# A hybrid diffusion layer: the first stage in two passes, scaled x times v0 and modulated x times v1

## The chip, the cores and the metric

The kernel runs on one core of a Trainium2 chip. The metric is the device time of one execution in microseconds; lower is better. All data is fp32; large products are split by hand into two parts of a rounded type, so each takes three products on TensorE (PE).

## The reference

One layer of a bidirectional backbone over 640 tokens (128 context tokens and 512 latent ones) of width 2048, with a conditioning vector for each of the two groups. The part in question is the beginning:

```python
sh1, sc1, g1, sh2, sc2, g2 = modulation(cond, w_mod, b_mod)    # silu(cond) @ w_mod + b_mod, cut into 6 pieces
u = rmsnorm(x, g_pre_mix) * (1.0 + sc1) + sh1
q, k, v, o, ig, fg, z, xbc, dt = split(u @ w_in)
```

After that come an mLSTM on four heads (it reads q, k, v and the gates ig, fg) and an SSD on 16 heads (it reads a 3x3 convolution of xbc, and dt), both in two directions over chunks of 128 tokens, an output projection, a second norm and modulation, and an MLP of width 8192 with squared ReLU.

## The kernel before, in words

Everything is kept with features on the partitions: x is 16 tiles k of 128 features x 640 tokens (`xT`, KT = 16). The modulated input u is held as `ah` (rounded) and `al` (what is left), so that a product is `ah*whi + ah*wlo + al*whi`. A weight block of 128x1024 (512 KB) is loaded by SyncE into `raw`, cast by ScalarE (ACT) into `whi` (L204), and its rest is formed by VectorE (DVE) into `wlo` (L205); `raw` has two buffers, `whi` and `wlo` three each.

The first stage (L293 to L353) does this:

- It loads x in eight DMAs of two tiles (L298), squares each tile on ACT (L300) and adds the squares on DVE into `rb` (L302). `norm_row` sums over partitions on PE, takes the root on GpSimd and spreads the result (L166 to L178, L304).
- `mod1(k)` (L315 to L330) makes scale and shift of tile k: two loads of 1 MB (L312), 16 products of 32x256 in four column groups of PE (L321), a copy (L325), two transposes and a sum (`mod_sum`, L258, L259), then scale `a1` (L329) and shift `modT` (L330).
- The loop over k (L335) forms u as x*a1*rb on DVE (L341), `ah` as u+shift on ACT (L342), `al` on DVE (L343), multiplies with the 48 gate columns (`mm_a` into `gps`, L217), and, after every second k, with two tiles of v0, the first 512 columns of v (`mm_b` into `vps`, L233 to L235: 30 products of 512 columns).

v0 and v1 are the two halves of v; v0 serves heads 0 and 1 of the mLSTM, v1 heads 2 and 3. After the stage the gate columns and v0 are copied out of PSUM (`gT` L404, `v_tile` L396), and the gate chain begins: small products on PE (L412 to L524) between many small operations on DVE and ACT, with a round trip through DRAM, up to `wk`, `dec` and `gu` (L509 to L512). Beside it PE does v1 by `proj_b` and q and k of head 0 by `proj_a`. Each weight block of those takes with it one `mod_step` (L261 to L279), which does a quarter of one of the other modulation pieces: a load into `mraw`, four products of 32x256 (L269), an addition. The mLSTM of head h (`mlstm`) begins with transposes of k (L590) and needs `wk` for `kw` (L593); q and k of the next head are projected beside it. The convolved tiles 8 and 12 of the SSD are projected between q, k of head 3 and its mLSTM.

The order on each engine is written out by a scheduler when the kernel is built, from the order of the program and the buffers of the pools; on the chip each engine follows it strictly.

## Time and profile before

| what | value |
| --- | --- |
| median of 3 runs | 2887.56 us (2886.55 to 2887.63) |
| profiled execution, its own time | 2888.12 us |
| its span in the profile | 2886.4 us, 48385 instructions |
| PE busy | 2833.0 us (98%) |
| DVE, ACT, POOL busy | 67%, 45%, 15% |
| granted TensorE clock, mean | 0.997 |
| DMA | 498.52 MB, mean 173 GB/s |

The page divides the span into 40 slices of 72 us. PE is full in all but the first, where it stands at 6 tenths; the DMA is at 9 tenths in that slice alone and in a short stretch late in the run. Products are pipelined, so a busy PE need not be at its peak: the time of a product is better read from the step between two starts than from its duration.

### The profile page before, as it was taken

The page shows a single profiled execution, that of the slowest core. Times are in us where ns is not written, and L with a number is a line of the kernel's source. Part 1 is how long each engine was busy: PE and PEld are TensorE (multiplying, and loading weights), DVE is VectorE, ACT ScalarE, POOL GpSimd, SP SyncE. Part 2 cuts the span into 40 slices and gives each one's busy share as a digit, 9 for nine tenths or more (in the row PEclk, how much of TensorE's full clock was granted, in tenths as well). Part 3 has the DMA queues.
Part 4 walks back from the last instruction along what each step waited for, and adds up shares of the span by engine and source line. Part 5 has one row for each costly group of instructions (what it writes and reads, how often), then busy time and mean ns, then how long its engine had stood idle before and what let it go on. Part 6 is the DMA issues. An engine that isn't in the chain of part 4 may idle for free.

```text
span 2886.4 us, 48385 instructions
## 1 busy us (share of the span) xinstructions
PE 2833.0 (98%) x18872; PEld 2631.7 (91%) x18872; DVE 1944.4 (67%) x3117; ACT 1286.1 (45%) x2312; POOL 419.3 (15%) x456
## 2 busy tenths in 40 slices
PE   6999999999999999999999999999999999999998
PEld 4679897888887889999999999999999999999997
DVE  4463464787765757677777666666776776677976
ACT  3322333233413423555444444444555556555364
POOL 0000000223211000000000000000005444443200
PEclk9999999999999999999999999999999999999999
DMA  9743434555647667555444333333448999997254
GB/s 364 291 137 115 141 120 134 176 167 159 207 144 226 240 228 264 206 182 168 161 158 138 113 108 114 110 109 108 163 128 182 213 204 191 196 214 178 88 208 157
DMA packets 211748, 498.52 MB, mean 173 GB/s; under 512 B 22424, under 2 KB 111768, under 8 KB 211008
## 3 DMA queue, kind: packets, MB, share of 16 engines
q1 hardware_dynamic: 153872, 429.38, 43.7%
q0 software_dynamic: 39792, 45.73, 10.1%
q10 hardware_dynamic: 17856, 20.32, 1.9%
q8 instruction: 148, 2.42, 0.3%
q14 instruction: 80, 0.66, 0.1%
HBM read 405.33 MB, written 44.97 MB: 156 GB/s over the span
## 4 chain that ended last, share of the span: by engine, by line
PE 92%; DVE 4%; DMA 3%; issue 1%; ACT 1%; DVEq 0%; SPq 0%; POOL 0%; ACTq 0%; POOLq 0%
PE mm L812 20%; PE mm L810 20%; PE mm L811 20%; PE mm L217 10%; PE mm L233 3%; PE mm L235 3%; PE mm L234 3%; PE tr L269 3%; PE mod L321 1%; DVE wlo L948 1%; PE vps L233 1%; DMA raw<-in_w 1%; PE vps L234 1%; PE ms L634 1%; PE vps L235 1%
## 5 line engine op out<-in xcount | busy, mean ns | idle before, releaser
L948 ACT CAST whi<-raw 128x512 fp32r<-128x512 f32 (+1 forms) x659 | 500.7, 767 | 584.1 <-PE mm L811 391.9
L948 DVE TENSOR_TENSOR wlo<-raw,whi 128x512 fp32r<-128x512 f32 (+1 forms) x659 | 574.8, 880 | 259.1 <-ACT whi L948 253.3
L810 PE MATMUL mm<-ah,whi 128*128 128x320 f32 x1536 | 477.8, 311 | 1.2 <-ACT whi L948 1.2
L812 PE MATMUL mm<-ah,wlo 128*128 128x320 f32 x1536 | 474.4, 310 | 4.2 <-DVE wlo L948 3.9
L811 PE MATMUL mm<-al,whi 128*128 128x320 f32 x1536 | 475.8, 310 | 0.0
L204 ACT CAST whi<-raw 128x1024 fp32r<-128x1024 f32 x162 | 169.3, 1047 | 405.9 <-PE mm L235 128.7
L810 PEld LDWEIGHTS mm<-ah,whi 128*128 128x128 f32 x1536 | 289.2, 188 | 9.8 <-issue 7.8
L812 PEld LDWEIGHTS mm<-ah,wlo 128*128 128x128 f32 x1536 | 288.6, 188 | 9.5 <-DVE wlo L948 4.7
L1229 POOL DMA_DIRECT2D pc<-ev x275 | 241.6, 905 | 365.2 <-ACT ev L1228 356.3
L811 PEld LDWEIGHTS mm<-al,whi 128*128 128x128 f32 x1536 | 289.2, 188 | 4.4 <-issue 4.1
L205 DVE TENSOR_TENSOR wlo<-raw,whi 128x1024 fp32r<-128x1024 f32 x162 | 202.0, 1248 | 132.3 <-ACT whi L204 131.9
L217 PE MATMUL mm<-ah,whi 128*128 128x256 f32 (+1 forms) x768 | 189.7, 319 | 0.0
L217 PE MATMUL mm<-al,whi 128*128 128x256 f32 (+1 forms) x768 | 188.9, 319 | 0.0
L217 PE MATMUL mm<-ah,wlo 128*128 128x384 f32 (+1 forms) x768 | 186.0, 316 | 0.0
L233 PE MATMUL mm<-whi,ah 128*128 128x512 f32 x400 | 161.6, 404 | 0.0
L234 PE MATMUL mm<-wlo,ah 128*128 128x512 f32 x400 | 160.0, 400 | 0.0
L235 PE MATMUL mm<-whi,al 128*128 128x512 f32 x400 | 159.5, 399 | 0.0
L810 PE MATMUL mm<-q,whi 128*128 128x320 f32 x512 | 157.7, 308 | 0.0
L812 PE MATMUL mm<-q,wlo 128*128 128x320 f32 x512 | 157.7, 308 | 0.0
L1228 ACT COPY ev<-mm 128x320 f32<-128x320 f32 x275 | 116.2, 425 | 65.4 <-DMA pc<-ev 46.2
L217 PEld LDWEIGHTS mm<-ah,whi 128*128 128x128 f32 x768 | 121.1, 188 | 10.2 <-issue 9.1
L217 PEld LDWEIGHTS mm<-ah,wlo 128*128 128x128 f32 x768 | 120.7, 188 | 6.9 <-issue 5.8
(419 smaller groups left out, 6692.6 us busy)
## 6 DMA issues: line engine op xcount, KB each, us to landing
raw<-in_w SPq DMA_DIRECT2D x460, 512.0 KB, 3.5
mraw<-in_w SPq DMA_DIRECT2D x128, 512.0 KB, 4.1
pc<-ev POOLq DMA_DIRECT2D x275, 160.0 KB, 4.9
m<-in_w SPq DMA_DIRECT2D x32, 1024.0 KB, 6.3
R<-hd SPq DMA_DIRECT2D x32, 640.0 KB, 7.0
xs<-csd SPq DMA_DIRECT2D x40, 256.0 KB, 5.0
hd<-s ACTq DMA_DIRECT2D x62, 160.0 KB, 2.9
hd<-u ACTq DMA_DIRECT2D x62, 160.0 KB, 1.9
```

The costliest lines, as they stand in the source:

```text
L204: S.copy(hi, t)
L205: V.tensor_sub(lo, t, hi)
L217: PE.matmul(ps[h][:, 0:HW[h]], lhsT=w[:, cs_], rhs=a[:, k, HS[h]], start=(k == 0 and i == 0), stop=(k == KT - 1 and i == 2))
L233: PE.matmul(ps[:, :], lhsT=ah[:, k, tok], rhs=hi[:, wc], start=first, stop=False)
L234: PE.matmul(ps[:, :], lhsT=ah[:, k, tok], rhs=lo[:, wc], start=False, stop=False)
L235: PE.matmul(ps[:, :], lhsT=al[:, k, tok], rhs=hi[:, wc], start=False, stop=last)
L810: PE.matmul(ps, lhsT=wh[:, c], rhs=bh[:, k, :], start=(start and k == 0), stop=False)
L811: PE.matmul(ps, lhsT=wh[:, c], rhs=bl[:, k, :], start=False, stop=False)
L812: PE.matmul(ps, lhsT=wl[:, c], rhs=bh[:, k, :], start=False, stop=(stop and k == nk - 1))
L948: newest[:] = S.copy(hi, src), V.tensor_sub(lo, src, hi)
L1228: S.copy(ev, ps)
L1229: G.dma_start(pi[:, j, :], ev, accum_op=OP.add)
```

## The change

The first stage becomes two passes over k, in pairs. Pass 1 needs only the scale: it multiplies x*a1, without the norm and without the shift, with v0, and the norm's factor of each token is put in when v0 leaves PSUM (`rc5`). The squares are formed in this pass, into one buffer. Pass 2 has the shift and the norm, forms u as before and multiplies it with v1; `ah` and `al` of all k come out of it for the later projections. The modulation blocks are laid out anew: a block row of 32 x 256 now holds 256 columns of scale (pass 1) or of shift (pass 2), loaded as four DMAs of 512 KB, with five buffers of `m1` and the two of `mraw`; x is loaded pair by pair. Shift's part of v0 is the same for all tokens of a group, so it is a product of the shift vector with the weights of v0: `v0_steps` loads the eight blocks of v0 a second time, forms it in steps that go beside the next projections (in place of `mod_step` there, which then runs later), and adds it to v0. The gate columns become a projection of their own after pass 2. The convolved tiles 8 and 12 are projected right after q and k of head 0. Line numbers with "L" in the rows of the change are its own.

```diff
@@ block_keys
-    for k in range(KT):
-        keys += [("m1", k, j) for j in range(4)]
-        if k % 8 == 0:
-            keys.append(("A", "g", 0, k // 8))
-        if k % 2 == 1:
-            keys.append(("B", "v", 0, k // 2))
-    keys += [("B", "v", 1, j) for j in range(8)]
+    for v in range(2):
+        for p in range(KT // 2):
+            keys += [("m1", v, p, j) for j in range(4)]
+            keys.append(("B", "v", v, p))
+    keys += [("A", "g", 0, j) for j in range(2)]
@@ proj_a, proj_b
-                if mod["n"] < MODCAP[0]:
-                    mod_step()
+                side_step()
...
+        def side_step():
+            if first:
+                if next(first[0], "end") == "end":
+                    first.pop()
+                else:
+                    return
+            if mod["n"] < MODCAP[0]:
+                mod_step()
...
-            for k in range(KT):
-                if k % 2 == 0:
-                    SY.dma_start(xT[:, k:k + 2, :], A["xT"][:, k * T:(k + 2) * T].rearrange("p (a b) -> p a b", b=T))
-                sq = rb if k == 0 else (wb, wp)[k % 2].tile([P, 1024], F32, tag=("raw", "mraw")[k % 2], name="sq", bufs=2)[:, 0:T]
-                S.activation(sq, xT[:, k, :], AF.Square)
-                if k:
-                    V.tensor_add(rb, rb, sq)
...
+            def load_m1(v, p):
+
                 r = []
-                for jj in range(2):
-                    w = p0.tile([P, 2, 1024], F32, tag="m1", name="m1", bufs=4)
...
+                for j in range(4):
+                    i = more["m1"] = more.get("m1", -1) + 1
+                    if i % 7 < 2:
+                        w = wp.tile([P, 1024], F32, tag="mraw", name="mraw", bufs=2)
+                    else:
+                        w = p0.tile([P, 1024], F32, tag="m1", name="m1", bufs=5)
+                    SY.dma_start(w, A["w"][BLK["m1", v, p, j]])
                     r.append(w)
                 return r
...
+            mod1(0, 0)
+            load_x(0)
+            for p in range(KT // 2):
+                vw = split_block(("B", "v", 0, p))
+                if p + 1 < KT // 2:
+                    load_x(p + 1)
+                    mod1(0, p + 1)
+                else:
+                    mod1(1, 0)
+                for k in (2 * p, 2 * p + 1):
+                    for ci, cc in enumerate(CC):
+                        S.activation(ah[:, k, cc], xT[:, k, cc], AF.Copy, scale=a1[:, k, ci:ci + 1])
+                        V.scalar_tensor_tensor(al[:, k, cc], xT[:, k, cc], a1[:, k, ci:ci + 1], ah[:, k, cc],
+                                               OP.mult, OP.subtract)
+                    sq = rb if k == 0 else p0.tile([P, T], F32, tag="u", name="sq", bufs=1)
+                    S.activation(sq, xT[:, k, :], AF.Square)
+                    if k:
+                        V.tensor_add(rb, rb, sq)
...
+                v_pair(vps, vw, p)
...
+            for t in range(NT):
+                if t % 2:
+                    V.tensor_scalar(v_out(vts[0], t), two_heads(vps[t]), rc5[:, t:t + 1], None, OP.mult)
+                else:
+                    S.activation(v_out(vts[0], t), two_heads(vps[t]), AF.Copy, scale=rc5[:, t:t + 1])
+
+            vps = [pv.tile([P, 512], F32, tag="v", name="vps", bufs=5) for _ in range(NT)]
+            for p in range(KT // 2):
+                vw = split_block(("B", "v", 1, p))
+                if p + 1 < KT // 2:
+                    mod1(1, p + 1)
...
+                v_pair(vps, vw, p)
...
+        def v0_steps():
+            w = []
+            for j in range(8):
+                w.append(raw_block(("B", "v", 0, j), "mraw"))
+                if j % 2:
+                    ps = trt()
+                    for g in range(4):
+                        k = 2 * j - 2 + g
+                        PE.matmul(ps[32 * g:32 * g + 32, :], lhsT=shT[:, k, :],
+                                  rhs=w[k // 2][:, k % 2 * 512:(k % 2 + 1) * 512], start=True, stop=True)
+                    if j == 1:
+                        V.tensor_copy(vpart, ps)
+                    else:
+                        V.tensor_add(vpart, vpart, ps)
+                if j < 7:
+                    yield
+            for c in range(2):
+                sel = gp.tile([P, P], F32, tag="vsel", name="vsel", bufs=2)
+                V.tensor_scalar(sel, ones, vcol[:, c:c + 1], None, OP.mult)
+                ps = trt()
+                PE.matmul(ps, lhsT=sel, rhs=vpart, start=True, stop=True)
+                for t in range(NT):
+                    if (t > 0) == c:
+                        V.tensor_add(v_out(vts[0], t), v_out(vts[0], t), two_heads(ps))
+
+        first[:] = [v0_steps()]
+        gT = fmt()[0:48, :]
+        for i, ps in enumerate(proj_a("g", 0)):
+            S.copy(gT[:, HS[i]], ps[0:48, 0:HW[i]])
...
-        vts.append(v_tile(proj_b("v", 1)))
         qk0 = qk(0)
+        pre = {}
+        for m in (8, 12):
+            pre[m] = fmt()
+            conv_tile(m, pre[m])
...
         qk3 = qk(3)
-        pre = {}
-        for m in (8, 12,):
-            pre[m] = fmt()
-            conv_tile(m, pre[m])
```

**ACT, opening.** ACT's queue from the first x tile to the second cast before (L300 squares, L204 casts):

```order
L300 ACTIVATE rb<-xT 128x640
L300 ACTIVATE sq<-xT 128x640 x15
L325 COPY part_218<-mod_201 128x256
L342 ACTIVATE ah<-u,modT 128x128
L204 CAST whi<-raw 128x1024
L342 ACTIVATE ah<-u,modT 128x512
L325 COPY part_248<-mod_231 128x256
L204 CAST whi<-raw 128x1024
```

With the change, from the first cast to the third (L384 squares, L380 `ah`, L345 the copy of a modulation sum, L202 casts):

```order
L202 CAST whi<-raw 128x1024
L384 ACTIVATE sq<-xT 128x640 x2
L202 CAST whi<-raw 128x1024
L384 ACTIVATE sq<-xT 128x640
L345 COPY part_189<-mod_172 128x256
L384 ACTIVATE sq<-xT 128x640 x2
L380 ACTIVATE ah<-xT,a_100 128x128
L380 ACTIVATE ah<-xT,a_100 128x512
L380 ACTIVATE ah<-xT,a_100 128x128
L380 ACTIVATE ah<-xT,a_100 128x512
L384 ACTIVATE sq<-xT 128x640 x6
L202 CAST whi<-raw 128x1024
```

The squares stood ahead of everything; now they stand between the casts and the `ah` of the first pairs, six of them ahead of the third cast.

**SyncE, opening.** Its loads before (L298 x, L312 modulation, L197 weights):

```order
L298 DMA xT<-in_xT 128x1280 x8
L312 DMA m_197<-in_w 128x2x1024
L312 DMA m_199<-in_w 128x2x1024
L312 DMA m_227<-in_w 128x2x1024
L312 DMA m_229<-in_w 128x2x1024
L197 DMA raw<-in_w 128x1024
```

With the change (L332 modulation, L357 x, L195 weights), to the third block of v0:

```order
L332 DMA mraw<-in_w 128x1024 x2
L332 DMA m_126<-in_w 128x1024
L332 DMA m_128<-in_w 128x1024
L357 DMA xT<-in_xT 128x1280
L195 DMA raw<-in_w 128x1024
L357 DMA xT<-in_xT 128x1280
...
L357 DMA xT<-in_xT 128x1280 x2
L332 DMA m_251<-in_w 128x1024
L357 DMA xT<-in_xT 128x1280 x2
L195 DMA raw<-in_w 128x1024
L332 DMA m_253<-in_w 128x1024
L332 DMA m_332<-in_w 128x1024
```

Modulation comes ahead of x, and all of x comes ahead of the third block of v0.

**PE, from the first stage to the first recurrence.** Before, at the end of the first stage (L217 gate columns, L235 with `vps` v0, L412 the first small gate product, L233 to L235 with `mm` v1):

```order
L217 MATMUL gps<-ah,wlo 128x384
L217 MATMUL gps<-ah,wlo 128x256
L235 MATMUL vps<-whi,al 128x512 x4
L412 MATMUL ms<-ident,fm 128x48 x5
L269 MATMUL tr<-mraw,scT 32x256 x4
L233 MATMUL mm<-whi,ah 128x512
L234 MATMUL mm<-wlo,ah 128x512
L235 MATMUL mm<-whi,al 128x512
```

With the change, from the end of pass 2 (L215 projections of gate columns, q, k and tiles 8 and 12; L483 and L495 shift's part of v0; L507, L598, L619 small gate products; L688 transposes of k for head 0):

```order
L232 MATMUL vps<-whi,al 128x512 x5
L215 MATMUL mm<-ah,whi 128x384
...
L483 MATMUL tr<-mraw,shT 32x512 x4
L215 MATMUL mm<-ah,whi 128x384
...
L507 MATMUL ms<-ident,fm 128x48 x5
L215 MATMUL mm<-ah,wlo 128x256
...
L495 MATMUL tr<-vpart,vsel 128x512
L598 MATMUL ms<-ident,fm 128x36
L619 MATMUL ms<-ident,csx 32x128 x4
L215 MATMUL mm<-ah,whi 128x256
...
L688 MATMUL ms<-ident,fm 128x128 x2
L215 MATMUL mm<-ah,whi 128x384
```

The small gate products followed the first stage and ran beside v1; now they follow the gate columns and run beside q, k and the two convolved tiles.

## Rows read from the trace of the kernel before

**Rows 1.** Busy us by stretch: PE, PEld, DVE, ACT, POOL; granted clock, DMA share, GB/s.

```profile
0.00:22.40 22.40, 0.00 (x0) 0.00 (x0) 13.72 (x24) 12.41 (x18) 1.21 (x8) 1.00 0.89 341
22.40:33.20 10.80, 10.47 (x54) 6.25 (x54) 2.67 (x12) 0.37 (x1) 1.57 (x2) 1.00 1.02 409
33.20:146.00 112.80, 107.88 (x844) 73.93 (x845) 54.65 (x127) 35.00 (x61) 1.46 (x2) 1.00 0.84 313
146.00:213.50 67.50, 66.47 (x348) 49.60 (x347) 47.54 (x127) 16.85 (x33) 2.16 (x3) 1.00 0.44 147
```

**Rows 2.** What PE waited for up to 141 us: total, times, longest.

```profile
PE nrm L166 <- DVE rb L302: 22.5, 1, 22.5
```

**Rows 3.** Timeline of ACT, then DVE, opening: start us, us, engine, line.

```profile
8.75 1.36 ACT L300 ACTIVATE sq<-xT 128x640 f32<-128x640 f32 x2 [0.23 <-DMA xT<-in_xT]
...
18.31 1.36 ACT L300 ACTIVATE sq<-xT 128x640 f32<-128x640 f32 x2 [0.22 <-DMA xT<-in_xT]
...
8.55 13.87 DVE L302 TENSOR_TENSOR rb<-rb,sq 128x640 f32<-128x640 f32 x15 [4.62 <-ACT sq L300]
```

**Rows 4.** Timeline of PE, one pair of k in the first stage.

```profile
100.18 1.07 PE L321 MATMUL mod<-m,scT 128*32 128x256 f32 x16
...
104.86 0.39 PE L233 MATMUL vps<-whi,ah 128*128 128x512 f32 x1
105.09 0.39 PE L234 MATMUL vps<-wlo,ah 128*128 128x512 f32 x1
...
107.49 1.93 PE L321 MATMUL mod<-m,scT 128*32 128x256 f32 x32 [0.27 <-DVE sm L259]
...
114.12 1.07 PE L321 MATMUL mod<-m,scT 128*32 128x256 f32 x16
```

**Rows 5.** Timeline of PE, one side step among the wide products.

```profile
155.77 0.64 PE L269 MATMUL tr<-mraw,scT 128*32 128x256 f32 x8
156.34 0.50 PE L233 MATMUL mm<-whi,ah 128*128 128x512 f32 x1
```

**Rows 6.** Chain that ended last: start us, us, what; q projection.

```profile
213.53 2.27 PE mm L217 x13
...
221.78 7.08 PE mm L217 x48
```

**Rows 7.** Groups by line and shape up to 141 us: busy us, mean ns, idle before.

```profile
L205 DVE TENSOR_TENSOR wlo<-raw,whi 128x1024 fp32r<-128x1024 f32 x11 | 13.5, 1223 | 6.6 <-ACT whi L204 6.6
...
L302 DVE TENSOR_TENSOR rb<-rb,sq 128x640 f32<-128x640 f32 x15 | 12.4, 825 | 6.1 <-ACT sq L300 4.6
L204 ACT CAST whi<-raw 128x1024 fp32r<-128x1024 f32 x11 | 11.5, 1041 | 7.4 <-PE vps L235 7.4
...
L342 ACT ACTIVATE ah<-u,modT 128x512 fp32r<-128x512 f32 x15 | 10.8, 721 | 3.4 <-DVE u L341 3.4
L300 ACT ACTIVATE sq<-xT 128x640 f32<-128x640 f32 x15 | 10.3, 728 | 1.6 <-DMA xT<-in_xT 1.6
...
L342 ACT ACTIVATE ah<-u,modT 128x128 fp32r<-128x128 f32 x15 | 6.0, 403 | 30.7 <-DVE u L341 30.3
L325 ACT COPY part<-mod 128x256 f32<-128x256 f32 x16 | 5.9, 369 | 43.7 <-PE mod L321 43.7
...
L329 DVE TENSOR_SCALAR a<-sm,b,par 128x2 f32<-128x2 f32 x16 | 4.6, 289 | 0.6
```

**Rows 8.** Timeline of PE, fp32 products of 257 columns in a recurrence.

```profile
277.57 0.59 PE L633 MATMUL ms<-St,qw 128*128 128x257 f32 x2
278.00 0.59 PE L634 MATMUL ms<-v,pT 128*128 128x257 f32 x2
```

**Rows 9.** Timeline of ACT, then PE: gate chain start, end, and first user.

```profile
146.42 0.73 ACT L404 COPY fm<-gps 48x384 f32<-48x384 f32 x2
...
201.74 0.24 ACT L509 ACTIVATE gu<-gu 128x40 f32<-128x40 f32 x1 [0.25 <-DVE gu L506]
...
248.77 0.38 PE L590 MATMUL ms<-ident,fm 128*128 128x128 f32 x2
```

More of the change, by code (lines that the diff above doesn't have):

```diff
@@ new lines, in build @@
+            mod1(0, 0)
[16 more added lines that the diff above has]
+                        V.tensor_add(rb, rb, sq)
+                if p == KT // 2 - 1:
+                    pt = pv.tile([P, 512], F32, tag="g", name="nrm", bufs=2)
+                    for i in range(NT):
+                        PE.matmul(pt[:, i:i + 1], lhsT=rb[:, i * P:(i + 1) * P], rhs=ones[:, 0:1],
+                                  start=True, stop=True)
+                    V.tensor_scalar(rc5, pt[:, 0:NT], 1.0 / D, EPS, OP.mult, OP.add)
+                    G.tensor_tensor(rc5, rc5, mhalf[:, 0:NT], OP.pow)
+                v_pair(vps, vw, p)
@@ new lines, in build @@
+            for i in range(NT):
+                V.tensor_scalar(rb[:, i * P:(i + 1) * P], ident, rc5[:, i:i + 1], None, OP.mult)
+            for c in CC:
+                pt = pv.tile([P, 512], F32, tag="g", name="nrm", bufs=2)
+                for i in range(c.start, c.stop, P):
+                    PE.matmul(pt[:, i - c.start:i - c.start + P], lhsT=ones, rhs=rb[:, i:i + P], start=True, stop=True)
+                S.copy(rb[:, c], pt[:, 0:c.stop - c.start])
+            for t in range(NT):
[3 more added lines that the diff above has]
+                    S.activation(v_out(vts[0], t), two_heads(vps[t]), AF.Copy, scale=rc5[:, t:t + 1])
```

102 lines of the change are left out of this document (53 added, 49 removed).

## The prediction

> **What bounds the kernel now.** I read the first 213.5 us in stretches, then what PE waited for, then single rows. Up to 22.4 us PE does nothing [rows 1]. It waits for one thing, the sum of squares of x on DVE [rows 2]: all eight double tiles of x are loaded first, one every 1.59 us (from 8.75 to 18.31 us in six steps), and 15 additions of 0.83 us follow one another until 22.4 us [rows 3]. From 33.2 to 146 us PE is busy 107.9 of 112.8 us while the DMA moves 313 GB/s, well under the 409 GB/s of the stretch before [rows 1]. One pair of k takes 13.94 us there, from 100.18 to 114.12 us [rows 4]. The work in a pair fills it: 30 wide products a step of 0.23 us apart make 6.9; 12 gate products at 0.1475 (48 in 7.08 [rows 6]) make 1.8; two modulation blocks at 1.93 and 0.2 for the switch [rows 4] make 4.3; two pairs of transposes at some 0.45 make 0.9. That is 13.9 us. So the long part of the stage is bound by PE, not by its loads, and only the opening is empty. The granted clock is 1.00 in all four stretches, its level of 2.4 GHz, the empty one included [rows 1], so the clock gives no term.
>
> **The account before.** At 213.5 us (the next product, for q, starts at 213.53 [rows 6]) PE has done 480 wide products (110.4 us), 96 gate products (14.2), 16 modulation blocks (34.1), their transposes (7.2) and the products of the norm (some 3). Of the last 67.5 us [rows 1], 240 wide products take 55.2 and eight side steps at 0.57 and 0.2 around it [rows 5], with one piece's transposes, 6.8; the 5.5 left I divide into 1.6 of waiting for emptied banks and 3.9 of small gate products. All work is 179.6 us, so 33.9 us are idle.
>
> **What the change does to it.** The same work remains: the eight side steps go to later projections, where PE is as full, so they are neither gained nor lost. New is shift's part of v0. Four groups of products of 32x512: four side by side with 256 columns take 0.57 [rows 5], so with 512 some 1.07 and 0.2 around, 5.1 in all. Two products of 128x512 in fp32: 257 columns step 0.43 [rows 8], so 0.86 and 0.2 each, 2.1. Together **7.2 us** of new PE work. The 4 MB loaded twice costs nothing where 147 GB/s flow [rows 1]. Additions to vpart and v0 on DVE lie beside the q and k projections.
>
> The idle time is what changes, and I replay the opening in the order of the rows shown above the prediction. SP issues four half-size modulation blocks first. At x's pace (640 KB in 1.59 us) a block takes 1.28 us: the fourth lands near 10.7, the first x at 12.3, v's first block at 13.6. Modulation ends at 11.3; copy 0.37, transposes some 0.45, their sum 0.2 and two scales of 0.29 [rows 7] give a1 at 13.0. But ACT does two squares (0.73 each) ahead, then four ah (2.24) and the cast (1.04) [rows 7]: first wide product at **17.1 us**, with 2.4 of work behind it, so 14.7 idle. Pair 0 has the next modulation block in four pieces between its products and ends near 27; pair 1 starts at 29 when its scales and first ah are there, and PE is through with it and the next block at 38.5. Then comes the weak place: SP has loaded all of x ahead of v's third block, and ACT has six squares in a row ahead of that cast. One buffer holds a square, so each waits for its addition: 0.73 and 0.83 and the hops, 1.65 [rows 7]. The cast ends at 41, the copy of the modulation sum at 42.1, pair 2 starts at 44.8. It ends at 53.3; the norm's columns, the next scales (the DVE has two wlo of 1.22 ahead) and a modulation block follow, and pair 3 starts at **57.4**. From 17.1 to 57.4 the work is 31.9 us, so 8.4 are idle or lost in split-up blocks.
>
> After that a pair costs PE 6.9 + 2.13 + 0.45 = 9.5 us; ACT needs 3.7 and DVE 6.4 (in the second pass two u, two al, wlo and the sums), and the loads 2.6 MB, 276 GB/s, less than the 313 the stage now carries: PE bounds both passes. Pass 1 ends near 105, pass 2 near 179, q starts near 196. Further idle: 0.5 where the banks of v0 are emptied (a modulation block of 2.1 lies between), 1.6 before the gate columns as now, and 1.0 for small gate products that come before DVE is done. Sum: 14.7 + 8.4 + 0.5 + 1.6 + 1.0 = 26.2 against 33.9, a gain of 7.7, less 7.2 new: **0.5 us faster**. The profiled execution took 2888.12, 0.56 above the median of the runs, so the forecast is 2887.1 us: no change. A measurement here can tell 0.2%, 5.8 us.
>
> The opening is the unknown price. If the squares hold nothing up, pair 2 follows pair 1 and 6 us more are gained. If the loads come at the 313 GB/s of the busy stretch [rows 1] instead of 410, all landings stretch by 1.31: the block on which pair 3 waits lands at 64 and not 50, and 7 us are lost. I take the middle, since the rows of x and of the second stretch, with nothing ahead of them, show 410 and 409.
>
> The Trainium skill, DMA: Bandwidth & Descriptors, section Bandwidth, speaks against the change: batch transfers to 1 MiB or more for 75% of peak, and this halves 1 MB loads into 512 KB ones. By it the opening would be that slower case, near 2894 us. The trace disagrees so far: transfers of 640 KB, several queued, kept 410 GB/s [rows 3], as the 1 MB ones did, 409 [rows 1].
>
> Moving the gate columns behind v1 and the two convolutions before the first recurrence keeps PE's sum. Today the gate chain runs from the copy at 146.42 to its last exponentials at 201.7, 55 us, and its first user on PE comes at 248.77 [rows 9]: 47 us of slack. Then the first user comes after 354 products (52.2), the new work, three side steps and the small products (2.3 and 3.9): 66 us behind the gate columns less the part of the 7.2 that lies beside them, so 63 to 66. The chain gains four additions to vpart and five to v0 of some 0.7 on DVE, 6 us: 61. It fits, narrowly.
>
> **Rivals.** (a) Faster: the squares do not hold the third cast, or the transfers run ahead of my landings; 6 to 8 us less, 2880. For it: DVE has room in the opening. Against: the order on ACT is fixed and one buffer holds the squares. (b) Slower, by the gate chain: it becomes the bound where it passes 63 us. If the taps of the two convolutions (some 20 of 0.75) stand in DVE's queue ahead of its end, it takes 61 + 15 and PE waits up to 13 us: 2900. Against: most of the taps come behind it in the order. (c) Slower, by the loads of the opening: 2894. (d) That it does not do what it says can be left out: PE starts with the modulation block, and no sum of squares stands ahead of it.
>
> **Numbers.** Forecast of no change 0.48. Faster by over 5.8 us: (a) 0.25. Slower: (b) 0.14, (c) 0.08, 0.05 for waits for banks or fm buffers in the recurrences, together 0.27. The range takes in (a) and (c) and part of (b): 2879 to 2897.
>
> **What would show it.** Right: first wide product near 17 us, the fourth pair near 57, pass 1 to 105, pass 2 to 179, q near 196, with pairs 9.5 us apart after the fourth, and no wait of PE on kw or the small gate products above 2 us. The forecast fails on the fast side if the fourth pair starts before 51; on the slow side if it starts after 63, if pairs in the passes are over 10 us apart, or if PE waits for ACT's kw at the first recurrence.

## The result, and the profile after

The changed kernel takes 2927.44 us (median of 4 runs, 2926.61 to 2928.32) against 2887.06 us of the kernel before, timed on the same chip (2886.53 to 2887.63): a ratio of 1.014, 95% interval 1.0122 to 1.0157. It is 40 us slower. The forecast was 2887.1 us, no change. One profiled execution has a span of 2926.2 us.

The page after, its head and its first part (busy us, share of the span, instructions):

```profile
span 2926.2 us, 48614 instructions
...
PE 2855.7 (98%) x18908; PEld 2639.3 (90%) x18908; DVE 1962.7 (67%) x3160; ACT 1299.3 (44%) x2346; POOL 420.9 (14%) x455
```

The four stretches of [rows 1] in the changed kernel (busy us of PE, PEld, DVE, ACT, POOL; granted clock, DMA share, GB/s):

```profile
0.00:22.40 22.40, 10.32 (x55) 4.40 (x56) 7.42 (x21) 7.76 (x13) 1.20 (x8) 1.00 0.89 334
22.40:33.20 10.80, 10.41 (x70) 5.79 (x69) 6.77 (x12) 5.76 (x10) 0.00 (x0) 1.00 1.02 411
33.20:146.00 112.80, 109.00 (x743) 77.31 (x742) 63.51 (x129) 46.46 (x82) 1.18 (x1) 0.97 0.81 299
146.00:213.50 67.50, 66.84 (x429) 56.64 (x428) 37.70 (x87) 17.91 (x30) 1.46 (x2) 1.00 0.41 150
```

The opening did what it was meant to: PE works 10.3 us of the first 22.4, where it did nothing before. What PE waits for up to 110 us, which answers to [rows 2] (total, times, longest), and the first wide product, in the chain of waits:

```profile
PE mod L341 <- DMA mraw<-in_w: 7.5, 1, 7.5
PE mod1t L254 <- ACT part L345: 3.7, 2, 3.1
PE vps L230 <- ACT whi L202: 3.5, 1, 3.5
```

```profile
17.06 2.50 PE vps L230 x5
```

So the 40 us are lost elsewhere. To find where, I take the same product in both traces and compare its start. Behind the z projection all wide products have one form (the two W_hi lines and the W_lo line of `mm3`, L810 to L812 before, L905 to L907 after): 512 of each line make the output projection, the rest the MLP. A number below is how much later the nth product of the W_lo line starts than in the kernel before, where the four start at 959.7, 1170.9, 1225.9 and 1725.6 us.

| start against the kernel before, us | 1st | 401st | 513th, first of the MLP | 1601st | modulation steps done by 950 us | last step at |
|---|---|---|---|---|---|---|
| before | 0 | 0 | 0 | 0 | 87 | 1206.3 |
| after | -2.7 | -1.6 | +49.3 | +36.7 | 75 | 1261.7 |

Up to 1170 us nothing seems lost. Then 51 us go in one place, between the last products of the output projection and the first of the MLP, and 13 come back, since MLP products that before ran among the waits of the second half's norm now run behind it, at full pace. From the 1601st product to the end 3 us more come, in part in small waits for cast weights (4.4 us on `wlo` against 2.6).

One trace tells such a difference to some 4 us and not better: up to the first of these products f5, g1 and f1 below are the same program as the change, and they stand at -1.0, -0.5 and +1.6 us where it stands at -2.7.

The place in stretches of 20 us, the kernel before and then the changed one (columns as in rows 1):

```profile
1220.00:1240.00 20.00, 20.00 (x139) 19.78 (x138) 11.76 (x20) 6.79 (x10) 0.85 (x1) 1.00 0.42 149
1240.00:1260.00 20.00, 20.00 (x112) 17.46 (x111) 14.32 (x14) 10.02 (x12) 0.00 (x0) 1.00 0.69 257
1260.00:1280.00 20.00, 20.00 (x137) 19.59 (x136) 14.63 (x31) 13.58 (x25) 0.85 (x1) 1.00 0.32 109
```

```profile
1220.00:1240.00 20.00, 13.48 (x102) 8.88 (x100) 10.42 (x23) 0.88 (x2) 0.85 (x1) 0.81 0.49 164
1240.00:1260.00 20.00, 15.84 (x72) 9.73 (x76) 9.65 (x17) 5.08 (x4) 0.85 (x1) 0.76 0.53 192
1260.00:1280.00 20.00, 8.92 (x40) 6.31 (x33) 18.87 (x30) 15.26 (x21) 0.00 (x0) 0.50 0.34 123
```

The timeline of PE there, in the changed kernel (start us, us, line; in brackets the idle time ahead and what ended it):

```profile
1235.06 1.08 PE L265 MATMUL tr<-mraw,scT 128*32 128x256 f32 x8
1241.23 1.08 PE L265 MATMUL tr<-mraw,scT 128*32 128x256 f32 x8 [5.10 <-DVE macc L271]
1243.94 9.49 PE L1013 MATMUL ms<-x,ones 128*128 128x320 f32 x24 [1.63 <-ACT x L1010]
...
1261.70 1.08 PE L265 MATMUL tr<-mraw,scT 128*32 128x256 f32 x8 [0.23 <-DMA mraw<-in_w]
1267.62 0.69 PE L254 MATMUL tr<-ident,macc 128*128 128x128 f32 x2 [4.84 <-DVE macc L271]
1272.03 0.63 PE L905 MATMUL mm<-ah,whi 128*128 128x320 f32 x1 [3.72 <-ACT whi L1043]
```

L265 are modulation steps, L1013 belongs to the norm of the second half, L905 at 1272 is the MLP. Steps that used to be over at 1206 run alone among the norm's products up to 1262, and no longer at 0.74 us each: the addition that ends a step stands in DVE's queue behind the norm's own operations, four in 5.7 us (L1007 is the norm's, L271 the step's):

```profile
1235.17 5.68 DVE L1007 TENSOR_TENSOR q<-q,ms 128x1280 f32<-128x1280 f32 x4 [1.34 <-PE ms L176]
1240.77 0.41 DVE L271 TENSOR_TENSOR macc<-macc,tr 128x256 f32<-128x256 f32 x1
```

The MLP begins behind the steps. The first two blocks of its weights are loaded at 1203.7 and 1207.9 us into the two `raw` buffers that stay; the buffers of all later ones lie in the memory of the steps' weights and sum, which is given free by `wctx.close()` behind `mod_to(128)`. SP's queue shows it (L1078 loads the MLP's weights; total, times, longest, from 1200 to 1300 us; then the loads in order of time):

```profile
SPq L195 <- PE tr L265: 37.7, 12, 9.2
...
SPq L1078 <- DVE macc L271: 4.4, 1, 4.4
SPq L1078 <- DMA mraw<-in_w: 3.4, 1, 3.4
...
SPq L1078 <- PE tr L265: 1.2, 1, 1.2
```

```profile
1256.44 1.72 SPq L195 DMA_DIRECT2D mraw<-in_w  x2
1262.83 17.79 SPq L1078 DMA_DIRECT2D raw<-in_w  x6
```

The third load waits for the landing of the last step's weights and for that step's products. The MLP's first cast on ACT comes at 1271.0, behind the last operations of the norm. It is so in all six kernels here that lose time between the 401st product and the 513th (the change, e2, e3, f1, f3, i3): the third load starts 0.7 to 1.1 us behind the last step, and the first cast 3 to 8 us behind that load. Where PE waits, the granted clock falls to 0.81, 0.76 and 0.50, the last of which is its level of 1.2 GHz.

Why are the steps late? One is issued beside each weight block, as long as some are left. Before, 88 blocks stood ahead of the output projection: v1 8, q and k 16, the convolutions 32, o 16, z 16. In the change v1 is in the first stage and issues none, the gate columns add 2, and the eight new blocks of v0 take the place of 7: 75. So 13 steps move into the output projection.

My theory (S) was then that these late steps are the whole loss. Its rivals: that it comes from what else moved (G: gate columns, convolutions, new products), and that the clock fell for a reason of its own (C).

### The profile page after: what moved, and what is told of

Same layout as the page of the kernel before. It is cut to its first block, busy times and chain, and to the rows that moved or that the text cites. A ratio compares the mean times of both kernels' runs of the same rounds, so it can differ in the third digit from the quotient of the medians.

```text
span 2926.2 us, 48614 instructions
## 1 busy us (share of the span) xinstructions
PE 2855.7 (98%) x18908; PEld 2639.3 (90%) x18908; DVE 1962.7 (67%) x3160; ACT 1299.3 (44%) x2346; POOL 420.9 (14%) x455
## 4 chain that ended last, share of the span: by engine, by line
PE 90%; DVE 4%; DMA 3%; issue 1%; ACT 1%; SPq 0%; POOL 0%; DVEq 0%; ACTq 0%; POOLq 0%
PE mm L907 20%; PE mm L905 20%; PE mm L906 20%; PE mm L215 11%; PE mm L231 3%; PE mm L232 3%; PE mm L230 3%; PE tr L265 2%; PE vps L230 1%; PE vps L231 1%; PE vps L232 1%; PE mod L341 1%; DMA raw<-in_w 1%; DMA R<-hd 1%; DVE wlo L1043 1%
## 5 line engine op out<-in xcount | busy, mean ns | idle before, releaser
L905 PE MATMUL mm<-ah,whi 128*128 128x320 f32 x1536 | 479.3, 312 | 4.1 <-ACT whi L1043 4.1
L907 PE MATMUL mm<-ah,wlo 128*128 128x320 f32 x1536 | 475.9, 311 | 6.0 <-DVE wlo L1043 5.9
L202 ACT CAST whi<-raw 128x1024 fp32r<-128x1024 f32 x162 | 169.4, 1047 | 376.6 <-PE mm L906 109.4
L905 PEld LDWEIGHTS mm<-ah,whi 128*128 128x128 f32 x1536 | 290.4, 189 | 13.2 <-issue 7.8
L907 PEld LDWEIGHTS mm<-ah,wlo 128*128 128x128 f32 x1536 | 289.8, 189 | 11.0 <-DVE wlo L1043 6.5
L906 PEld LDWEIGHTS mm<-al,whi 128*128 128x128 f32 x1536 | 290.4, 189 | 4.9 <-issue 4.9
L215 PE MATMUL mm<-al,whi 128*128 128x384 f32 (+1 forms) x800 | 199.5, 319 | 0.0
L215 PE MATMUL mm<-ah,whi 128*128 128x384 f32 (+1 forms) x800 | 198.1, 319 | 0.7 <-DVE v L458 0.7
L215 PE MATMUL mm<-ah,wlo 128*128 128x384 f32 (+1 forms) x800 | 197.0, 317 | 0.0
L905 PE MATMUL mm<-q,whi 128*128 128x320 f32 x512 | 158.1, 309 | 0.0
L907 PE MATMUL mm<-q,wlo 128*128 128x320 f32 x512 | 158.1, 309 | 0.0
L215 PEld LDWEIGHTS mm<-ah,whi 128*128 128x128 f32 x800 | 126.9, 189 | 11.2 <-issue 8.9
L215 PEld LDWEIGHTS mm<-al,whi 128*128 128x128 f32 x800 | 127.4, 189 | 7.6 <-issue 6.4
L215 PEld LDWEIGHTS mm<-ah,wlo 128*128 128x128 f32 x800 | 126.9, 189 | 4.4 <-issue 3.3
L232 PE MATMUL mm<-whi,al 128*128 128x512 f32 x320 | 130.6, 410 | 0.0
L231 PE MATMUL mm<-wlo,ah 128*128 128x512 f32 x320 | 130.0, 406 | 0.0
```

What stands on the lines that cost most here:

```text
L202: S.copy(hi, t)
L215: PE.matmul(ps[h][:, 0:HW[h]], lhsT=w[:, cs_], rhs=a[:, k, HS[h]], start=(k == 0 and i == 0), stop=(k == KT - 1 and i == 2))
L231: PE.matmul(ps[:, :], lhsT=ah[:, k, tok], rhs=lo[:, wc], start=False, stop=False)
L232: PE.matmul(ps[:, :], lhsT=al[:, k, tok], rhs=hi[:, wc], start=False, stop=last)
L905: PE.matmul(ps, lhsT=wh[:, c], rhs=bh[:, k, :], start=(start and k == 0), stop=False)
L906: PE.matmul(ps, lhsT=wh[:, c], rhs=bl[:, k, :], start=False, stop=False)
```

## The experiments

**Thirteen steps withheld in the kernel before.**

```diff
                 hi, lo = split_block(("B", name, n, j))
-                if mod["n"] < MODCAP[0]:
+                if mod["n"] < MODCAP[0] and name != "v" and not (name == "z" and n == 0 and j < 5):
                     mod_step()
```

> The kernel before, whose eight blocks of the second value projection and first five z blocks issue no modulation step, nothing else changed: the same 13 steps late. Theory S: the loss appears in the old kernel too, at the same place: 2920 to 2935 us, the second half's norm chain without TensorE work under it. Rivals G and C: as the kernel before, 2885 to 2892.

Measured: 2918.04 us, ratio 1.0108 (1.0093 to 1.0123). The first product behind z starts 9.6 us early (13 steps of 0.74 us not yet done), the MLP's first 39.4 late, the 1601st 27.0; the last step runs at 1252.4. The old kernel shows the same wait at the same place:

```profile
1220.00:1240.00 20.00, 11.00 (x65) 5.91 (x65) 15.29 (x23) 5.32 (x5) 0.85 (x1) 0.66 0.63 204
1240.00:1260.00 20.00, 11.86 (x72) 6.83 (x70) 11.27 (x27) 7.03 (x15) 0.85 (x1) 0.81 0.47 168
```

Late steps alone make a loss of 31 us, a little under the 2920 to 2935 of theory S and far from the rivals' range. The mechanism is shown, its size is not that of the change.

**The last twelve steps left out of the change.** `MODCAP` and the last `mod_to` stop at 116 in place of 128.

> The changed kernel without its last twelve modulation steps (their six columns of the last scale stay zero, so the output lacks them). Theory S: the lateness of these steps is the whole loss at the end of the output projection; what is left is the stretch ahead of it, where the changed kernel stood 1.6 us ahead of the kernel before at the 400th of the products behind z, with twelve fewer steps done: 2884 to 2889 us. If the loss at the start of the MLP is the norm chain's own, or the MLP's weight buffers in whatever memory: 2905 or more.

Measured: 2891.28 us, ratio 1.0007 (0.9997 to 1.0016). That is 2 us above what was expected. The MLP's first product starts 0.8 us behind the kernel before. The stretches of the loss are full again:

```profile
1220.00:1240.00 20.00, 20.00 (x139) 19.78 (x138) 11.59 (x21) 7.57 (x11) 0.85 (x1) 1.00 0.46 149
1240.00:1260.00 20.00, 20.00 (x113) 17.62 (x113) 14.98 (x13) 10.02 (x12) 0.00 (x0) 1.00 0.66 234
1260.00:1280.00 20.00, 20.00 (x135) 19.43 (x134) 13.97 (x27) 12.89 (x23) 0.85 (x1) 1.00 0.36 128
```

Neither the norm chain nor the clock nor the MLP's start has a fault of its own: C falls. But this kernel has 8.9 us of steps (12 by 0.74) less to do and is no faster than the kernel before, so something ahead of the output projection costs about as much. G is not out.

**Steps given back earlier, in five kernels.** In `side_step`, seven steps are no longer displaced by v0's (e3); six second steps in o and z on top of that (e1); thirteen second steps in o and z (e4), in the convolutions (f4), or in every other of the first 26 blocks of the output projection (f1).

```diff
-                else:
-                    return
```

```diff
                 hi, lo = split_block(("B", name, n, j))
                 side_step()
+                if name in ('o', 'z') and j % 2 and more["x"] < 13:
+                    more["x"] += 1
+                    side_step()
```

> The changed kernel with its 13 missing side steps given back ahead of the output projection: a shift step of v0 no longer takes a modulation step's place (7), and six of the o and z blocks issue two (6). Theory S (the side steps come too late: the burst of them stands alone behind the output projection and holds the memory of the MLP's weights): the last step falls where it fell before the change, no wait of over 10 us around 1230 to 1275, and the 40 us go: 2880 to 2887 us, since the changed kernel was 3 us ahead at the second half's norm. Rival G (the 40 us come from what moved in the opening: gate columns, convolutions, the added products): 2920 to 2930, as the change. Rival C (TensorE's clock fell for a reason of its own between 1243 and 1315): the clock stays at half there, 2905 or more.

> The changed kernel, only the seven displaced steps given back: the last modulation step falls at the fourteenth part of the second half of the output projection rather than at the eighth (before) or the twenty-first (the change). Theory S: six steps of some 4 us late against a slack of about 25 us (1206 to 1231 in the kernel before): nearly all of the loss is gone, 2882 to 2896 us; 2903 to 2908 would mean that the cost is proportional to the steps and has no slack. Rivals G and C: 2920 to 2930.

> The changed kernel with v0's shift steps left in the places they took, and thirteen blocks of the o and z projections issuing two modulation steps instead. Theory S: what counts is how many steps are issued ahead of the output projection and not which block issues them: 2880 to 2888 us, as with the steps given back early. If two steps in a block cost TensorE what it can't hide, some 0.4 us for each of the 13 more: up to 2893. Rivals G and C: 2920 to 2930.

> The changed kernel with a second modulation step in every other of the first 26 blocks of the output projection. Theory S, with a step priced at the 0.74 us of TensorE that thirteen withheld steps gave the kernel before ahead of the output projection (9.6 us): no wait behind the output projection, and the kernel then stands -2.7 + 9.6, some 7 us behind the kernel before: 2892 to 2897 us. Rival D (the steps are bound by their loads and buffers, which are as busy there as they can be): the stall stays or moves into the output projection, 2905 to 2920.

> The same thirteen steps as second steps of the convolutions' second blocks. Theory S: 2892 to 2898 us, as in the output projection. Rival (as the o and z blocks showed: a second step in a block holds the one bank and the two weight buffers, and the blocks' other work waits): 2908 to 2920, with the loss ahead of the z projection.

| run | us | ratio, interval | 1st | 401st | 513th | 1601st | last step at |
|---|---|---|---|---|---|---|---|
| e1, 7 + 6 in o and z | 2919.16 | 1.0111 (1.0095 to 1.0126) | +27.6 | +30.7 | +30.8 | +30.1 | 1237.0 |
| e3, 7 early | 2915.08 | 1.0095 (1.0078 to 1.0112) | +5.8 | +7.5 | +23.6 | +21.6 | 1237.7 |
| e4, 13 in o and z | 2915.75 | 1.0097 (1.0082 to 1.0112) | +22.8 | +25.1 | +26.1 | +26.2 | 1238.7 |
| f1, 13 in the output projection | 2920.68 | 1.0115 (1.0098 to 1.0132) | +1.6 | +4.9 | +48.9 | +32.8 | 1263.3 |
| f4, 13 in the convolutions | 2929.85 | 1.014 (1.0119 to 1.0161) | +38.6 | +42.2 | +39.7 | +39.9 | 1226.2 |

By their times alone, all lie nearer to rival G's 2920 to 2930 than to theory S, and two of the five in it. The columns say otherwise. In e1, e4 and f4 the loss at the MLP is gone (the 401st and the 513th are late by the same within 2.5 us), and a new one of 23 to 39 us stands ahead of the output projection. It is not z that is late: its last product comes at 959.9, 947.4 and 949.5 us (955.8 in the change). But the last SSD product comes at 961.5, 958.2 and 967.7 us (898.1 in the change), and PE has little beside what follows it. Here is e4, then the change, from 950 to 1000 us:

```profile
950.00:1000.00 50.00, 41.15 (x258) 27.79 (x255) 38.77 (x85) 16.44 (x30) 8.14 (x8) 0.69 0.81 262
```

```profile
950.00:1000.00 50.00, 49.86 (x347) 43.01 (x345) 43.13 (x85) 24.80 (x41) 3.26 (x5) 1.00 0.65 225
```

A step shares its one PSUM bank with transposes of the SSD; that this is what holds the SSD back I only argue. In f1 the steps were asked for earlier and did not run earlier (74 by 950 us and 120 by 1226, where the change has 75 and 119; the last at 1263.3); that their two weight buffers set this pace I argue too. And in e3, six steps late still cost 16 us (from +7.5 to +23.6), so the slack of 25 us that I had read from 1206 and 1231 was not there. What the steps hold is not the norm at 1231 but the MLP's third load, and the first cast behind it comes at 1219.2 in the kernel before. With 3.2 us for the load and 0.7 from the step to it I estimate a slack of 1219.2 - 1206.3 - 3.9, some 9 us. It fits the columns: the lateness of the last step against the 401st product, less 9, is 15, 15, 41, 43, 46 and 48 us in e3, f3, i3, f1, e2 and the change, and these lose 16, 15, 42, 44, 48 and 51 us between the 401st and the 513th. In e1, e4, f4 and f5 the lateness stays under 9, and they lose 1 us or nothing. Theory S missed in all five: I had priced a step by TensorE alone a second time. The other readings named for f1 (the steps' own bound) and f4 (the other work of the blocks waits) were right in kind; in size f1 lies at the end of its range and f4 10 us above it, and f4's loss stands behind z and not ahead of it.

**Shift's part of v0 left out.** The line `first[:] = [v0_steps()]` goes, and six second steps stand in the output projection.

> The changed kernel without the shift's part of v0 (its eight loads, 32 products, four sums and ten additions are left out, so v0 and the output lack that term), six second steps in the output projection making up for the rest. Theory S and my price of the new products: 7 us less than the run with thirteen in the output projection, 2885 to 2890. If the added part costs more than its TensorE work (through its loads or the bank it shares): 2880 or less. If the new part was hidden: as that run, 2892 to 2897.

Measured: 2901.12 us, ratio 1.0045 (1.0028 to 1.0062), and its first product behind z starts 5.6 us early, 7.2 ahead of f1 and 2.9 ahead of the change; these two are the same program up to there. 80 steps are done by 950 us against 74 and 75, so 4.4 or 3.7 us (6 or 5 by 0.74) come on top: the part costs some 7 to 12 us, all of it and not its products alone. The forecast of 7.2 lies at the lower end. The time itself missed: steps are late here too, the last at 1226.3, and the MLP starts 11.5 us behind.

**Steps beside the MLP, and the convolutions.** The last 16 steps of the change run among the MLP's first products, with weights in the MLP's own buffers (g1); on top of that, the squares of the opening on GpSimd (g2), or the convolutions of tiles 8 and 12 back at their old place ahead of the last mLSTM head (g4). The last 12 steps of the kernel before beside the MLP (h1).

```diff
+            if mod["n"] < 128:
+                mod_step()
             next(fl, None)
```

```diff
-                    S.activation(sq, xT[:, k, :], AF.Square)
+                    G.tensor_tensor(sq, xT[:, k, :], xT[:, k, :], OP.mult)
```

> The changed kernel, but modulation steps stop at the 112th until the MLP begins; the last sixteen run among the MLP's first products, with weights in the MLP's own raw buffers and a small sum and condition tile of their own, so that the MLP's weight buffers wait for no step. Theory S: the loss at the end of the output projection goes; the steps' 0.74 us each (9 to 12 us) stay, partly in the 5 us that TensorE waited there in the kernel before: 2886 to 2896 us. Rival D (the steps' loads delay the MLP's weights, which use the same buffers): 2900 or more, with TensorE waiting for whi in the first products of the MLP.

> The run before (steps beside the MLP) with the sixteen squares of x in the opening on GpSimd in place of ScalarE. If ScalarE's squares, which wait one by one for VectorE's additions and stand ahead of the next modulation's eviction, are what held TensorE at 39 to 46 us and led to the half clock at 52 to 59: 4 to 9 us less than that run. If the loads at 410 GB/s set the pace there: the same within 2 us. If GpSimd, at about 2.1 us for a square (1.69 us for 512 columns elsewhere), is late for the norm: 2 to 6 us slower.

> The run with the steps beside the MLP, and the convolutions of tiles 8 and 12 back ahead of the last mLSTM head (the last two steps of the shift's part of v0 then run right behind the first q and k). If the move of the two convolutions is worth nothing: within 3 us of that run. If their early place costs the 4 us more of TensorE waits between 400 and 800 that the changed kernel showed: 3 to 6 us less. If it hides the gates' chain, as the change may have meant: 3 to 15 us more.

> The kernel before with its last twelve modulation steps beside the MLP's first products in the same way. Theory S: the steps were in time there, so their move is worth only the waits that they can fill around the second norm chain (5.1 us of TensorE idle and a half clock of 6.8 us between 1225 and 1350): 2880 to 2888 us. Slower, 2890 or more, if the MLP's own loads are delayed.

| run | us | ratio, interval | 1st | 401st | 513th | 701st | 1601st |
|---|---|---|---|---|---|---|---|
| g1 | 2915.37 | 1.0092 (1.0077 to 1.0107) | -0.5 | +0.5 | -1.3 | +23.6 | +25.4 |
| g2 | 2919.74 | 1.0109 (1.0094 to 1.0124) | +3.1 | +4.7 | +3.1 | +26.6 | +28.3 |
| g4 | 2904.16 | 1.0055 (1.0039 to 1.0072) | -10.3 | -8.1 | -12.2 | +11.1 | +11.4 |
| h1 | 2900.9 | 1.0041 (1.0027 to 1.0056) | -0.4 | -4.5 | -9.6 | +10.4 | +10.7 |

The MLP's start (the 513th) holds, and the loss comes a little later: between it and the 701st product sixteen steps cost 25 us and twelve 20, over twice their work, and PE waits for the MLP's own casts and for the steps' sums. PE's waits in g1 from 1226 to 1400 us:

```profile
PE mm L907 <- DVE wlo L1043: 8.2, 4, 5.4
PE tr L265 <- DVE macc L271: 2.7, 2, 2.2
PE mm L905 <- ACT whi L1043: 2.6, 5, 1.0
```

Rival D was right for g1 and h1, in part. g2 was 4 us slower than g1, as the last of its three expectations has it (GpSimd took 1.57 us for a square, and PE then waited 4.2 us for the sums of a modulation on VectorE). The find is g4: the two convolutions back at their old place are worth 11 us, more than any of the three expectations gave, and nearly all of it ahead of the output projection (-10.3 against -0.5).

**The convolutions alone, and both undone.** i3: the change with the two convolutions back. i4: the kernel before with them early. i1: i3 with all twelve missing steps given back, six by not displacing them and six as second steps of the later q and k blocks.

```diff
         qk0 = qk(0)
-        pre = {}
-        for m in (8, 12):
-            pre[m] = fmt()
-            conv_tile(m, pre[m])
+        for _ in first.pop():
+            pass
...
         qk3 = qk(3)
+        pre = {}
+        for m in (8, 12):
+            pre[m] = fmt()
+            conv_tile(m, pre[m])
```

> The changed kernel with the convolutions of tiles 8 and 12 back ahead of the last mLSTM head, and nothing else (the shift's last two steps run right behind the first q and k; twelve modulation steps are as late as in the change). If the move of the convolutions costs by itself (pair of runs beside the MLP: 2915 against 2904): 9 to 12 us less than the change, 2914 to 2919, with the second norm chain as bare as in the change. If that pair differed for its steps beside the MLP: 2924 to 2930.

> The kernel before with the convolutions of tiles 8 and 12 moved up behind the first q and k, as in the change, and nothing else. If their early place costs by itself: 2894 to 2900, with TensorE waits between 470 and 800 that the kernel before does not have. If it costs only together with the change's other work there (v1 and the shift's part): 2885 to 2890.

> The changed kernel with both undone: the convolutions in their old place, and all twelve missing modulation steps given back early (six where the shift's steps took their places, six as second steps of the later q and k blocks). Account: the kernel with the convolutions back stood 10.3 us ahead of the kernel before at the first product behind z with twelve steps undone; these cost 0.74 to 1.2 us each, 8.9 to 14.4; so it stands between 1.4 us ahead and 4 behind, with no late step: 2885 to 2892 us. If a second step in a block still holds the one bank (as in o, z and the convolutions): 2900 to 2920.

| run | us | ratio, interval | 1st | 401st | 513th | 1601st | last step at |
|---|---|---|---|---|---|---|---|
| i3, change, convolutions back | 2910.07 | 1.0078 (1.0063 to 1.0093) | -8.8 | -6.4 | +35.9 | +19.8 | 1250.3 |
| i4, before, convolutions early | 2905.99 | 1.0062 (1.0045 to 1.0078) | +16.1 | +18.7 | +17.2 | +17.3 | 1215.2 |
| i1, both undone | 2893.68 | 1.002 (1.0011 to 1.003) | +1.5 | +3.7 | +2.2 | +1.5 | 1200.2 |

All three missed their ranges: i3 gained more than expected, i4 lost more, and i1 lies 2 us above. The early place of two convolutions costs the kernel before 17 us by itself. Why, the products of the projections show. Here are those alone (the line of `mm_a`), the kernel before and then i4 (busy us of PE and PEld, granted clock, DMA share, GB/s):

```profile
420.00:440.00 20.00, 17.59 (x99) 14.59 (x98) 1.00 0.47 159
440.00:500.00 60.00, 0.53 (x4) 0.27 (x2) 1.00 0.38 124
```

```profile
420.00:440.00 20.00, 11.40 (x65) 9.54 (x63) 1.00 0.41 132
440.00:500.00 60.00, 0.00 (x0) 0.00 (x0) 1.00 0.30 93
500.00:540.00 40.00, 20.50 (x121) 19.28 (x122) 0.96 0.58 187
```

In the kernel before the projections pause at 440 us and the last recurrence product comes at 482: 42 us in which the recurrences run alone. In i4 the projections pause at 434 and the recurrences end at 511, 77 us; in the change 417 and 495, 78. From the first transposes of k to the last recurrence product the four heads take 233 us in the kernel before (249 to 482) and 235 in i4 (276 to 511), with or without the two convolutions' products among them, 28 us of work (192 products, at 7.08 us for 48 [rows 6]). So in the kernel before these products were free over this stretch. Taken out of it they are paid for: i4 is 29 us late at the end of the recurrences (511 against 482). At the first product behind z 16 are left; how the other 13 come back no experiment here tells. In the changed kernel they are free in part only: with them (i3) the four heads take 243 us, and 233 without (262 to 495). All the same PE is shown busy there, 60.00 of 60.00 us before and in i4 (i4's line, then its next stretch; columns as in rows 1):

```profile
440.00:500.00 60.00, 60.00 (x279) 48.82 (x281) 25.73 (x62) 15.96 (x33) 2.65 (x3) 1.00 0.30 93
500.00:540.00 40.00, 35.31 (x217) 28.82 (x213) 15.75 (x45) 18.47 (x46) 6.05 (x9) 0.96 0.58 187
```

279 small products in 60 us count as a full PE: the busy time has no room in it to see that nothing wide runs. Only the count and the line filter tell.

i1 nearly closes the account: the MLP starts 2.2 us behind the kernel before and the run is 5 us slower. So some 35 of the 40 us are the convolutions and the late steps, not the two passes. The 5 that stay, 3.6 of them by the medians behind the 1601st product, are open (the profiled execution, the slowest of ten, loses 8.9 there). The parts don't add up simply: alone in the kernel before they cost 31 and 17, together in the change some 35. Of the 17 us that i3 gains on the change 6 lie ahead of the output projection, and most of the rest behind it, since its last step comes at 1250 and not at 1262.

**The squares of the opening.** i1, and each square on ScalarE issued behind the eviction of the next modulation product.

```diff
-                    S.activation(sq, xT[:, k, :], AF.Square)
+                    with tc.issue_after(evict[0].ins):
+                        S.activation(sq, xT[:, k, :], AF.Square)
```

> The run before, and each square of the opening held behind the eviction of the next modulation product on ScalarE, so that no square stands ahead of it. If the squares held TensorE there (3.7 us for the eviction, 3.5 for the cast behind it, and the half clock that followed at 52 to 59, 3.4 us): 4 to 9 us less than that run, below the kernel before. If the loads at 410 GB/s set the pace: the same within 2 us. If the norm comes late for it: 2 to 6 us more.

Measured: 2893.46 us, ratio 1.0014 (1.0005 to 1.0024), the same as i1. The half clock lies at 40 to 50 us by the windows, not at 52 to 59 as I had put it, and it is gone. The change, then i5:

```profile
35.00:40.00 5.00, 4.42 (x31) 2.60 (x29) 2.48 (x3) 2.32 (x4) 0.00 (x0) 1.00 1.03 410
40.00:45.00 5.00, 2.06 (x18) 0.89 (x18) 4.05 (x7) 3.93 (x7) 0.00 (x0) 0.63 1.03 410
45.00:50.00 5.00, 5.00 (x25) 3.39 (x21) 3.90 (x7) 2.64 (x5) 0.00 (x0) 0.69 1.02 409
```

```profile
35.00:40.00 5.00, 4.64 (x32) 3.03 (x30) 1.23 (x1) 1.29 (x2) 0.00 (x0) 1.00 1.03 411
40.00:45.00 5.00, 3.67 (x32) 1.93 (x33) 3.95 (x9) 4.11 (x8) 0.00 (x0) 1.00 1.03 410
45.00:50.00 5.00, 5.00 (x27) 3.47 (x27) 1.34 (x2) 1.20 (x3) 0.00 (x0) 1.00 1.03 410
50.00:55.00 5.00, 4.41 (x44) 2.71 (x43) 3.70 (x8) 2.78 (x7) 0.00 (x0) 1.00 1.02 406
```

PE no longer stands still for long and keeps its clock. By the time alone this is the second of the three expectations, that the loads set the pace. The starts of the pairs say otherwise. The third, fourth and fifth pairs start at 42.8, 54.3 and 63.6 us, where i1 has 45.3, 59.0 and 69.4, and the eighth at 91.4 against 97.2: the squares did hold the opening, by 5.8 us, while the loads went on at 410 GB/s. But the second pass begins at 107.1 us, in i1 at 106.5. Held behind the evictions, the last square runs at 93.5 us, and the norm's sum (L394) and root (L397) stand behind the last pair of pass 1, where i1 has them at 55.4 and 56.8. The emptying of v0's banks and the first `u` of pass 2 wait for them. From i5:

```profile
98.76 1.17 PE L394 MATMUL nrm<-ones,rb 128*128 128x1 f32 x10
100.22 2.09 POOL L397 TENSOR_TENSOR rc<-rc,mhalf 128x5 f32<-128x5 f32 x1 [98.34 <-DVE rc L396]
```

So the first expectation and the third came true together and nearly cancel: 1.3 us of the gain are left at the second pair of pass 2.

**The first wait of the kernel before.** Its first modulation product ahead of the norm's products on TensorE, nothing of the change.

> The kernel before, whose first modulation product (16 products, about 1.9 us) stands ahead of the norm's products on TensorE rather than behind them, with the loads in the same order; nothing of the change. Its weights are there by some 16 to 17 us (2.6 MB of x and 2 MB of weights at about 410 GB/s from 5 us), while TensorE waits until 22.5. If the opening of the kernel before was bound by the chain squares, norm, first modulation, first eviction: the first wide product comes 2 to 4 us earlier and the kernel ends at 2882 to 2886 us, below both. If the loads behind it set the pace: 2886 to 2890.

Measured: 2887.62 us, ratio 0.9995 (0.9986 to 1.0004). The first product of v0 comes 3.5 us earlier (34.4 against 37.9), as the first of the two expectations has it, and 1.6 us are left at the first product behind z, but the end can't be told from the kernel before. The modulation product waits for its weights until 21.27 us, not 16 to 17:

```profile
21.27 1.93 PE L319 MATMUL mod<-m,scT 128*32 128x256 f32 x16 [21.27 <-DMA m<-in_w]
```

So the wait of 22.5 us in [rows 2] named the sums on VectorE, but the loads were only a microsecond ahead of them. Up to 22.4 us the kernel before was thus bound by its loads almost as much as by the sums. No version here beats it.

## Why the prediction was wrong, point by point

**The opening was right, mechanism and times.** The first products of the pairs start at 17.1, 30.3, 45.5, 58.9, 69.3, 78.6, 87.8 and 97.1 us; the second pass begins at 106.4, the gate columns at 176.4, q at 192.6. The cast behind six squares, the cause that I named for the slow third pair, is the one in the trace, and its price of 6 us measured 5.8 (i5). i1, with the convolutions and the late steps undone, stands 1.5 us behind the kernel before at the 1601st product, against 0.5 ahead by my sum, within what one trace can tell. Two readings did not hold. That the empty opening of the kernel before waits for the sums alone was half of it (j1). And the clock, for which I had no term, fell where PE waited, in the opening and behind the output projection; no run gives its share of the loss by itself.

**Failed: "the eight side steps go to later projections, where PE is as full, so they are neither gained nor lost."** They are thirteen (v1's 8 less the gates' 2, and 7 displaced by v0's own), and I priced them by TensorE's time alone, which was right at 0.74 us. I did not ask when the last of them is due. It is due ahead of the second half's norm, because the MLP's weights take the steps' memory, and the products that cover that norm need these weights. Nor did I ask what a late step costs among the norm's operations. Left out, twelve steps give back 36 us (2927.44 to 2891.28), 8.9 of them their own work.

**Failed: "moving … the two convolutions before the first recurrence keeps PE's sum."** It keeps the sum and takes cover away. I followed only the gate chain through this move, and it did fit: no wait of PE for it above 2 us, the first transposes of k at 261.8. What the convolutions had covered, the last head's recurrence, I did not look at: 17 us in the kernel before (i4).

**Right, at the lower end: the new products,** 7.2 us forecast and some 7 to 12 measured for the whole part (f3). **Right: the loads,** rival (c): 411 GB/s with 512 KB transfers in the second stretch, against 409 with 1 MB [rows 1]. The Trainium skill, DMA: Bandwidth & Descriptors, section Bandwidth, asks for 1 MiB or more; the trace again does not bear out a loss by halving them here.

**The rivals.** (a) needed the squares to hold nothing; they held what I said. And (a) would not have brought its 6 to 8 us: freed of the squares, as i5 does it, the opening gains 5.8 us and the norm takes nearly all of them back at the border of the passes. (b) and (c) did not happen. The rival that did was not on my list, though the profile had both halves of it: the last steps at 1206 and the norm at 1231, and the 42 us without a wide product at the end of the mLSTM.

## What to carry to other kernels

When a change moves small work that another loop carries along, count the carriers ahead of its due point before and after, and find what that due point releases (memory counts as much as data); the price of a step on the bound engine says nothing about it. A wide product beside a recurrence can be free, and part of it is paid for once it is moved out (17 of 28 us here), and a busy share of 100% doesn't show which of the two stretches one looks at: filter by the wide products' line. A run whose time stays the same can hide a gain and a loss that cancel: compare the starts of the same products along the way. And when late small work is to be caught up, it has its own bound (buffers, one bank), so issuing it twice as often may do nothing, or hold up what shares the bank.

## What the runs showed that I had not expected

- TensorE's granted clock fell to its level of 1.2 GHz in the opening after a wait of 3.1 us for one eviction (0.63 and 0.69 as means of 40 to 45 and 45 to 50 us), and stayed at 1.00 once the squares stood behind that eviction (i5). Behind the output projection it stood at 0.50 from 1260 to 1280 us, after 0.81 and 0.76 in the two stretches before, which had waits.
- GpSimd squares 128x640 in 1.57 us, faster than the 2.1 I had scaled from 1.69 us for 512 columns of another operation, and it still delayed VectorE's queue enough to lose 4 us.
- A step placed a second time in a block costs 1.2 us in the early q and k blocks (8.5 us for 7 in e3, -2.7 to +5.8) and 2 to 3 in o, z and the convolutions (25.5 us for 13 in e4, 41.3 in f4), for 0.74 us of work.
